# State-space and dilated block on one Trainium2 core: six projections as plain float32 products, by halves of the heads

## The chip, the cores and the metric

The program runs on one core of one Trainium2 chip. The metric is the device time of one execution in microseconds. TensorE (PE) multiplies matrices and loads its weights beside that (PEld); VectorE (DVE), ScalarE (ACT) and GpSimd (POOL) work on elements; SyncE (SP) issues the loads of the weights.

## What is computed

A first block (gated recurrence, attention, routed experts) is followed by a second block of two layers. The change lies in the first layer of the second block. For 256 tokens `x` of 1024 features that layer computes:

```python
h = rmsnorm(x, pre_norm[layer])
proj = h @ w_in                      # 1024 x 5120
q, k, v, g_att, u_ssm, g_ssm = jnp.split(proj, cuts, axis=-1)   # 4 x 1024, 2 x 512
q = apply_partial_rope(q, pos) * HEAD_DIM ** -0.5    # 16 heads of 64
k = apply_partial_rope(k, pos)
att = dilated_attention(q, k, v)     # causal; keys at offsets of three dilations; one softmax
ssm = s5_ssm(u_ssm, ...)             # 32 groups of 16 channels, 64 complex states each, then a GLU
merged = jnp.concatenate([att * silu(g_att), ssm * silu(g_ssm)], axis=-1)
x = x + rmsnorm(merged @ w_out, post_norm[layer])
```

## The kernel before

The layer is written in `even2` (from line 2062). Weights come by `wload` (line 169) as chunks `wch` of 1 MB: four blocks of 128 rows by 512 columns, two chunks for a projection of 512 columns. `rows` takes them to `split` (line 175) by halves of a chunk: ACT casts the half to float32r, the high part `wh` (line 188), and DVE subtracts it from the weight, the low part `wl` (line 189). The input is in two parts as well, `h` high and low, made by `gain_T` (line 456): ACT multiplies the transposed tokens by the gain (line 467), DVE makes the rest. `mm3` (lines 209 to 211) then forms high x high, high x low and low x high. `proj2` (line 2043) gives 512 columns by feature: 96 products of 128 weight columns by 256 tokens, named `pj`. `tokm` (line 221) gives 512 columns by token: 48 products of 512 columns, named `pv`.

The layer begins with `gain_T`, the sums of squares of the norm, and the two projections of the state space (columns 4096 and 4608). Then `ssm` (line 2195) goes through four groups `q` of four steps `j`. In a step PE forms `bu` (line 2213), DVE turns it by the rotation table of the group (lines 2218 to 2221: m1 and m2) and scans it (line 2225: z), and POOL turns it back (lines 2227 and 2228). m1, m2 and z are buffers of one ring, tag t2, of `t2b` = 10. At a group's end PE forms `yps` (line 2234), DVE `sy` (line 2236), ACT the gelu. When all four are done, `gl` (line 2241) is a product with unsplit weights, 16 of 128 x 128 by 256.

The rotation tables lie in four units `Eu[0..3]` of 8 KB a partition, one for each group. After the state space the same units hold the queries, keys, gates and values of all 16 heads, one kind in each unit. The attention goes by halves of the heads (`s`): queries and keys (projected, copied by ACT at line 2127, rotated by DVE and POOL in `rope`, line 737), values (ACT, line 2133), gate (DVE line 2108, silu on ACT), then `dil_pair` (line 2145) for four pairs of heads: scores `sd` (line 2154), mask and maximum on DVE, exp on ACT (line 2168), transposes (line 2180), `ob` (lines 2187 and 2191), and the gated result in two parts `ma`. The output product `yo` follows.

The code is written in this order, and a scheduler sets the order of each engine from what depends on what: products of later projections are issued between those of the state space and of the pairs of heads.

Of the kernel before, what the change touches and what calls it, by code (L numbers as in the profile page):

```python
# [20 lines left out]
P = 128  # L21
# [10 lines left out]
def _consts():  # L32
    """Tables that depend on shapes alone."""
# [53 lines left out]
class Kern:  # L87
# [32 lines left out]
    def consts(self):  # L120
        """what is not needed at the start"""
# [12 lines left out]
        # per token and expert: the token's number in two parts, the weight in three  # L134
# [12 lines left out]
    def unit(self, name, dt=F32):  # L147
        """a unit held from here on, in the order of the loads"""
        t = self.W.tile([P, 2048], dt, name=name, tag="w")
        if dt == F32:  # L150
            o = LAY["half"][0]
            with self.nc.allow_non_contiguous_dma("small"):
                self.nc.sync.dma_start(t[:, :1], self.a["const"][:, o:o + 1])
        else:
            self.nc.gpsimd.tensor_copy(t[:, :1], self.ident[:, :1])
        return t
# [18 lines left out]
    def split(self, v, perm=False, to=None):  # L175
        """f32 [P,k,c] -> two float32r parts whose sum is v; perm: columns (g a d) -> (a g d); to: where they go"""
# [15 lines left out]
    def rows(self, W, K, c0, cn=512, perm=False, got=()):  # L192
        """weight columns c0:c0+cn, row chunk by row chunk (k, high, low); got: loads that are under way"""
# [19 lines left out]
    def feat(self, outs, W, K, c0, x, xs, cn=512, perm=False, chk=False, it=None):  # L213
        """outs[i][128 columns, tokens] = W[:, c0 + 128 i ...].T @ x; x(k) -> high, low [P, tokens]"""
# [6 lines left out]
    def tokm(self, outs, W, K, c0, x, ts, cn=512, chk=False):  # L221
        """outs[i][128 tokens, columns]"""
# [7 lines left out]
    def rsqrt(self, v, shape, scale=1.0):  # L230
        """scale * v**-0.5 of a small tile: a guess on the exponent, then steps of the third and the second order"""
# [17 lines left out]
    def rstd_rows(self, tiles, n, junk):  # L249
        """1/sqrt(mean of squares + eps) of the rows of token tiles; junk: places for the squares, by halves of rows"""  # L250
# [12 lines left out]
    def rstd_of(self, ss, m, n=D):  # L263
        """from the sums of squares of the rows' halves [P, m, 2]"""
# [5 lines left out]
    def squares(self, t, c):  # L270
        """sums of squares of a half of the rows of tile t, for the second layer's norm"""
# [3 lines left out]
    def row_squares(self, ss, tiles, after=None):  # L275
        """ss[:, t, c]: the sums of squares of the halves of the tiles' rows"""
# [6 lines left out]
    def transpose_to(self, src, n, evac):  # L283
        """src(c) [P,128] for c<n, four a bank; evac(q, bank)"""
# [7 lines left out]
    def split_evac(self, hi, lo, src, eng=0):  # L292
        """src (PSUM or SBUF f32) -> hi + lo"""
# [38 lines left out]
    def ada_group(self, layer, i, bank=False):  # L332
        """generator: one weight chunk a step"""
# [43 lines left out]
    def ada_first_setup(self):  # L377
        """gains and shifts of the first norm: their biases, by feature"""
# [10 lines left out]
    def ada_first(self, f):  # L389
        """shift and scale of the features' quarter f for the first norm, both conditions; the row chunks' sums lie in  # L390
        four column groups"""
# [39 lines left out]
    def norm_turn(self, xs, dg, q, tag, bufs):  # L431
        """two row chunks of two token tiles: the transpose, times the row's factor"""
# [16 lines left out]
    def first_rows(self, it, n, pool=True):  # L449
        """the first weights of a phase, split beside the end of the one before"""  # L450
# [5 lines left out]
    def gain_T(self, xs, A, hT, banks, after=None):  # L456
        """x * gain of two token tiles, transposed, in two parts; the rows' factor comes to what the products give"""
        nc = self.nc
        for k in range(8):
# [8 lines left out]
            self.last_lo = nc.vector.scalar_tensor_tensor(lo, src, A[:, k:k + 1], hi.bitcast(F32), op0=OP.mult, op1=OP.subtract).ins  # L468

    def along(self, r, tag, bufs):  # L470
        """the rows' factors r [P, 2] of two token tiles along the free dimension, in every partition"""
# [11 lines left out]
    def router_prep(self, layer, NT):  # L483
        """the router's weights times the gain, what the shift adds, and the rows of shift and gain"""
# [24 lines left out]
    def router_half(self, c, lp, order):  # L509
        """transposes, products and sums of squares of the columns' half c; order: pairs of tiles"""  # L510
# [21 lines left out]
    def x_gain(self):  # L532
        """x * gain"""
# [7 lines left out]
    def router_end(self, lp):  # L541
# [16 lines left out]
        # the experts' affinities  # L558
# [4 lines left out]
    def layer0(self):  # L563
        nc, tc, a = self.nc, self.tc, self.a
        with ExitStack() as st:
# [25 lines left out]
            # by quarters of the features: the first projection's first row chunks wait for the first quarter alone  # L591
# [6 lines left out]
            def quarter(f):  # L598
                """its modulation, and its features of x, transposed"""
# [27 lines left out]
            # the units that the projections fill  # L627
# [66 lines left out]
            # output projection  # L694
# [42 lines left out]
    def rope(self, xv, cos, sin, half=16, eng=None, sin_eng=None):  # L737
        """eng, sin_eng: where the products with the cosines and the sines are done"""
# [22 lines left out]
    def lower_bounds(self):  # L761
        """of layer 0: the first softmax weight of three; and 1 - it, it - 1"""
# [18 lines left out]
    def hgrn(self, HU, v, Y, S2, more):  # L781
# [9 lines left out]
        for h in range(4):  # L791
# [3 lines left out]
            for d in range(2):  # L795
# [31 lines left out]
                # within chunks  # L827
# [5 lines left out]
                # keys by token  # L833
# [5 lines left out]
                # states before each chunk, in the order of the scan  # L839
# [43 lines left out]
    def head_norm(self, y, gain, eng):  # L883
        """rms_norm over each head's 128 columns, in place"""
# [61 lines left out]
    def route(self, NT, CB):  # L946
        """from the logits: each token's two experts, their weights and its rows among them"""
# [3 lines left out]
        # sel: the experts by groups, and the groups' scores behind them  # L951
# [1420 lines left out]
```

## Time and profile before

| | |
|---|---|
| median of 3 runs | 2246.64 us (2244.28 to 2251.62) |
| profiled execution: span (its own time is given by this alone) | 2244.3 us |
| mean granted clock | 0.957 |
| PE busy | 2015.4 us (90%) x11562 |
| PEld busy | 1382.0 us (62%) x11563 |
| DVE busy | 1461.3 us (65%) x2625 |
| ACT busy | 926.2 us (41%) x1377 |
| POOL busy | 340.3 us (15%) x376 |
| `even2` | from 1785 to 2062 us of the span |

The span runs from the first to the last instruction of one profiled execution. Busy time is the time in which an engine has an instruction at work; products overlap in their modelled ends, so the distance between the starts of two tells more than their length. The granted clock is the share of full speed that PE was given. Products of plain float32 leave two records each.

### The profile page before, as it was taken

Reading aid. Unit: us, or ns where it says so; the run is one execution under the profiler, and the core shown is the slowest. Engines: PE = TensorE matmul, PEld = TensorE weight load, DVE = VectorE, ACT = ScalarE, POOL = GpSimd, SP = SyncE. Lnnn points to the kernel's source line nnn. Section 1 sums busy time; section 2 is a strip of 40 time slices with the busy share of each in tenths; the row PEclk is TensorE's granted clock in tenths of the full one; section 3 lists DMA queues with packets and bytes.
Section 4 is the critical chain, followed back from the end, with each engine's and each line's share of the span. In section 5 each row is a group of like instructions: output and inputs, shape, how many; then the busy total and the mean of one; then the engine's idle time right before and its main releaser. Section 6 shows DMA issues by size and latency. Waiting matters only on the chain. (4 is left out here: it accounts for less than half of the span.)

```text
span 2244.3 us, 30379 instructions
## 1 busy us (share of the span) xinstructions
PE 2015.4 (90%) x11562; PEld 1382.0 (62%) x11563; DVE 1461.3 (65%) x2625; ACT 926.2 (41%) x1377; POOL 340.3 (15%) x376
## 2 busy tenths in 40 slices
PE   6997899969999999996989979999888788998998
PEld 2675675647778888774785533333333256786997
DVE  3336778668999999898857545232321288776767
ACT  2222324327778887774645610000000131555443
POOL 1210003040000000016020020011100035221111
PEclk9998999979999999999998989999999978999999
DMA  8854245649999999996532589999999922544560
GB/s 269 276 189 160 70 146 197 241 147 343 367 363 391 382 387 386 381 348 231 188 114 57 208 316 355 395 409 409 409 409 408 366 69 67 188 151 158 167 210 19
DMA packets 187068, 580.53 MB, mean 259 GB/s; under 512 B 18592, under 2 KB 41568, under 8 KB 181792
## 3 DMA queue, kind: packets, MB, share of 16 engines
q1 hardware_dynamic: 172416, 550.02, 66.2%
q0 software_dynamic: 7760, 23.26, 3.3%
q10 hardware_dynamic: 6736, 5.21, 0.8%
q8 instruction: 93, 1.52, 0.3%
q14 instruction: 63, 0.52, 0.1%
HBM read 568.41 MB, written 10.03 MB: 258 GB/s over the span
## 5 line engine op out<-in xcount | busy, mean ns | idle before, releaser
L189 DVE TENSOR_TENSOR wl<-wch,wh 128x1024 fp32r<-128x1024 f32 x534 | 676.3, 1286 | 155.2 <-ACT wh L188 139.4
L188 ACT CAST wh<-wch 128x1024 fp32r<-128x1024 f32 x540 | 562.0, 1052 | 377.8 <-PE pj L210 78.3
L211 PE MATMUL pj<-h,wl 128*128 128x256 f32 x512 | 148.2, 292 | 4.1 <-DVE wl L189 4.1
L209 PE MATMUL pj<-h,wh 128*128 128x256 f32 x512 | 148.7, 292 | 2.5 <-DVE ug L2301 1.2
L210 PE MATMUL pj<-h,wh 128*128 128x256 f32 x512 | 148.7, 291 | 0.0
L1265 PE MATMUL G<-wch,xT 128*64 128x512 f32 x512 | 125.8, 618 | 1.5 <-DMA wch<-in_moe_w_gate_dram 1.2
L1265 PE MATMUL U<-wch,xT 128*64 128x512 f32 x512 | 119.9, 600 | 4.1 <-DMA wch<-in_moe_w_up_dram 3.5
L1279 ACT ACTIVATE s<-G 128x512 f32<-128x512 f32 x16 | 9.6, 597 | 272.7 <-PE G L1265 272.7
L1265 PE MATMUL Y<-wch,hTe 128*64 128x512 f32 x488 | 110.5, 597 | 6.6 <-DMA wch<-in_moe_w_down_dram 5.0
L210 PE MATMUL U<-wl,xu 128*128 128x512 f32 x256 | 103.3, 403 | 9.6 <-DVE wl L189 8.6
L210 PE MATMUL G<-wl,xu 128*128 128x512 f32 x256 | 103.0, 402 | 8.3 <-DVE wl L189 8.0
L210 PE MATMUL Y<-wl,hu 128*128 128x512 f32 x256 | 102.9, 402 | 6.1 <-DVE wl L189 5.8
L211 PEld LDWEIGHTS pj<-h,wl 128*128 128x128 f32 x512 | 99.7, 196 | 9.6 <-DVE wl L189 4.7
L209 PE MATMUL U<-wh,xu 128*128 128x512 f32 x256 | 101.8, 397 | 3.4 <-ACT wh L188 3.4
L209 PEld LDWEIGHTS pj<-h,wh 128*128 128x128 f32 x512 | 100.6, 197 | 6.9 <-issue 3.1
L210 PEld LDWEIGHTS pj<-h,wh 128*128 128x128 f32 x512 | 100.6, 197 | 3.8 <-issue 3.6
L209 PE MATMUL Y<-wh,hu 128*128 128x512 f32 x256 | 100.6, 393 | 2.6 <-ACT wh L188 2.4
L209 PE MATMUL G<-wh,xu 128*128 128x512 f32 x256 | 101.4, 396 | 0.0
L211 PE MATMUL Y<-wh,hu 128*128 128x512 f32 x256 | 100.8, 394 | 0.0
L211 PE MATMUL U<-wh,xu 128*128 128x512 f32 x256 | 100.7, 393 | 0.0
L211 PE MATMUL G<-wh,xu 128*128 128x512 f32 x256 | 100.2, 391 | 0.0
L1232 POOL DMA_INDIRECT xg<-h2d,idx x15 | 18.7, 1244 | 419.3 <-PE tp L1236 403.9
(667 smaller groups left out, 4279.9 us busy)
## 6 DMA issues: line engine op xcount, KB each, us to landing
wch<-in_moe_w_gate_dram SPq DMA_DIRECT2D x128, 1024.0 KB, 7.7
wch<-in_moe_w_up_dram SPq DMA_DIRECT2D x128, 1024.0 KB, 9.0
wch<-in_moe_w_down_dram SPq DMA_DIRECT2D x125, 1024.0 KB, 7.7
wch<-in_ada_w_dram SPq DMA_DIRECT2D x40, 1024.0 KB, 6.0
wch<-in_even_w_in_dram SPq DMA_DIRECT2D x34, 1024.0 KB, 5.6
wch<-in_odd_w_in_dram SPq DMA_DIRECT2D x16, 1024.0 KB, 5.5
wch<-in_even_w_out_dram SPq DMA_DIRECT2D x10, 1024.0 KB, 6.3
wch<-in_ada_w_dram SPq DMA_DIRECT2D x32, 256.0 KB, 6.6
```

Of the source, the lines that this page charges most:

```text
L188: self.last_h = nc.scalar.copy(h, v).ins
L189: self.last_l = e.tensor_tensor(l, v, h.bitcast(F32), op=OP.subtract).ins
L209: m(out, lh, rh, start=first, stop=False, skip_group_check=chk)
L210: m(out, lh, rl, start=False, stop=False, skip_group_check=chk)
L211: self.last_m = m(out, ll, rh, start=False, stop=last, skip_group_check=chk).ins
L1232: nc.gpsimd.indirect_dma_start(out=xg[:], out_offset=None, in_=h2d[:, :], in_offset=bass.IndirectOffsetOnAxis(ap=idx[:, e:e + 1], axis=0))
L1265: self.last_m = nc.tensor.matmul(out[f * 64:f * 64 + 64, :], x[:, k, :], v[k - k0][:, f * 512:(f + 1) * 512], start=(k == 0), stop=(k == 7 ...
L1279: self.last_s = nc.scalar.activation(s, G, AF.Silu).ins
```

## The change

A method `plain` forms the projection by feature from unsplit chunks, a method `plain_tok` the one by token. Their input is `xw`, the transposed tokens times the gain in one float32 part, which `gain_T` makes with one more ACT instruction for each of eight blocks. `xw` takes 8 KB a partition, and the ring t2 has 9 buffers instead of 10. The two projections of the state space and the output product stay split. Each half of the heads now has two units of its own: queries and keys in `Eu[2s]`, values and gate in `Eu[2s + 1]`. The code's order is: queries of half 0, values and gate of half 0, queries of half 1, pairs 0 to 3, values and gate of half 1, pairs 4 to 7. (The two units `ma` are taken after the queries of half 1.) `dil_pair` indexes its unit by `jl = j % 4`.

```diff
+    def plain(self, outs, W, K, c0, x):
+        for k0 in range(0, K, 4):
+            v = self.wload(W, k0, 4, c0, 512)
+            for k in range(4):
+                for i, o in enumerate(outs):
+                    self.nc.tensor.matmul(o, v[:, k, i * P:(i + 1) * P], x[:, k0 + k], start=k0 + k == 0 and not i % 2, stop=k0 + k == K - 1,
+                                          skip_group_check=True)
+    def plain_tok(self, outs, W, K, c0, x):
+        for k0 in range(0, K, 4):
+            v = self.wload(W, k0, 4, c0, 512)
+            for k in range(4):
+                for t, o in enumerate(outs):
+                    self.nc.tensor.matmul(o, x[:, k0 + k, t * P:(t + 1) * P], v[:, k], start=k0 + k == 0, stop=k0 + k == K - 1)
...
-    def gain_T(self, xs, A, hT, banks, after=None):
+    def gain_T(self, xs, A, hT, banks, after=None, whole=None):
...
             self.last_lo = nc.vector.scalar_tensor_tensor(lo, src, A[:, k:k + 1], hi.bitcast(F32), op0=OP.mult, op1=OP.subtract).ins
+            if whole is not None:
+                nc.scalar.mul(whole[:, k], src, A[:, k:k + 1])
...
-            self.t2b = 10
+            self.t2b = 9
...
-            self.gain_T(xs, self.fpg, hT, (("tp", 1), ("bu", 2), ("bu", 2), ("pj", 4), ("pj", 4)), self.last_h)
+            xw = wk.tile([P, 8, 256], F32, name="xw", bufs=1)
+            self.gain_T(xs, self.fpg, hT, (("tp", 1), ("bu", 2), ("bu", 2), ("pj", 4), ("pj", 4)), self.last_h, xw)
...
             self.ssm(uT, gs, ms)
-            qT, kT, ga = (v8(self.Eu[i]) for i in range(3))
-            v = self.Eu[3].rearrange("p (t c) -> p t c", t=2)
+            def plain2(c0):
+                b = [ps.tile([P, 2, 256], F32, name="pj", tag="pj", bufs=4) for _ in range(2)]
+                self.plain([b[i // 2][:, i % 2] for i in range(4)], W, 8, c0, xw)
+                return b
+            def queries(s):
+                u = v8(self.Eu[2 * s])
+                for c0, dst in ((0, u[:, :4]), (1024, u[:, 4:])):
+                    for i, b in enumerate(plain2(c0 + s * 512)):
+                        nc.scalar.copy(dst[:, 2 * i:2 * i + 2], b)
+                        for m in range(2):
+                            self.rope(dst[:, 2 * i + m], cosb, sinb, half=8, eng=nc.gpsimd, sin_eng=nc.gpsimd)
+                return u[:, :4], u[:, 4:]
+            def values(s):
+                u = self.Eu[2 * s + 1]
+                v, ga = u[:, :1024].rearrange("p (t c) -> p t c", t=2), v8(u)[:, 4:]
+                o = [ps.tile([P, 512], F32, name="pv", tag="pj", bufs=4) for _ in range(2)]
+                self.plain_tok(o, W, 8, 2048 + s * 512, xw)
+                for t in range(2):
+                    nc.scalar.mul(v[:, t], o[t], rf[:, 2 + t:3 + t])
+                for i, b in enumerate(plain2(3072 + s * 512)):
+                    g = scaled(ga[:, 2 * i:2 * i + 2], b)
+                    nc.scalar.activation(g, g, AF.Silu)
+                return v, ga
+            h0 = queries(0) + values(0)
+            qk = queries(1)
             ma = [v8(self.unit("ma%d" % i, F32R)) for i in range(2)]
-            for s in range(2):
-                for c0, dst in ((0, qT), (1024, kT)):
-                    for i, b in enumerate(self.proj2(x, W, 8, c0 + s * 512, "pj", 4)):
...
-                for j in range(s * 4, s * 4 + 4):
-                    self.dil_pair(j, qT, kT, v, ga, dil, ma)
+            for j in range(4):
+                self.dil_pair(j, *h0, dil, ma)
+            h1 = qk + values(1)
+            for j in range(4, 8):
+                self.dil_pair(j, *h1, dil, ma)
```

Where the order of the engines moves, three places are shown. The first is ACT at the gain stage, before (`wh` is a cast of weights, `h_14963` the high part of the input, `sq` and `sqg` the squares of the norms):

```order
L188 CAST wh<-wch 128x1024 x2
L467 ACTIVATE h_14963<-tp,fpg 128x256 x7
L188 CAST wh<-wch 128x1024
L467 ACTIVATE h_14963<-tp,fpg 128x256
L281 ACTIVATE sq,nss<-xin 128x512 x4
L188 CAST wh<-wch 128x1024
L2089 ACTIVATE sqg,nss<-sqg 128x512 x4
L188 CAST wh<-wch 128x1024 x3
```

The same place now:

```order
L188 CAST wh<-wch 128x1024 x2
L485 ACTIVATE h_14963<-tp,fpg 128x256 x3
L488 ACTIVATE xw<-tp,fpg 128x256
L485 ACTIVATE h_14963<-tp,fpg 128x256
L488 ACTIVATE xw<-tp,fpg 128x256 x3
L485 ACTIVATE h_14963<-tp,fpg 128x256 x3
L488 ACTIVATE xw<-tp,fpg 128x256
L485 ACTIVATE h_14963<-tp,fpg 128x256
L488 ACTIVATE xw<-tp,fpg 128x256 x3
L298 ACTIVATE sq,nss<-xin 128x512 x4
L188 CAST wh<-wch 128x1024
L2110 ACTIVATE sqg,nss<-sqg 128x512 x4
```

Eight instructions for `xw` have come in, and the third cast, which stood before the last part of the input, stands behind the first squares.

The second place is DVE in the state space, at a border between two groups (m, z and sy as above), before:

```order
L2218 TENSOR_TENSOR m_15447<-bu,rotE_12498 128x512
L2219 TENSOR_TENSOR m_15448<-bu,rotE_12498 128x512
L189 TENSOR_TENSOR wl<-wch,wh 128x1024
L2220 TENSOR_TENSOR m_15447<-m_15447,m_15448 128x256
L2221 TENSOR_TENSOR m_15447<-m_15447,m_15448 128x256
L2225 SCALAR_TENSOR_TENSOR z<-rho,m_15447 128x256 x2
L2218 TENSOR_TENSOR m_15481<-bu,rotE_12500 128x512
L189 TENSOR_TENSOR wl<-wch,wh 128x1024
L2219 TENSOR_TENSOR m_15482<-bu,rotE_12500 128x512
L2236 SCALAR_TENSOR_TENSOR sy<-ug,dsk,yps 128x256
```

And now:

```order
L2257 TENSOR_TENSOR m_15456<-bu,rotE_12498 128x512
L2258 TENSOR_TENSOR m_15457<-bu,rotE_12498 128x512
L2259 TENSOR_TENSOR m_15456<-m_15456,m_15457 128x256
L2260 TENSOR_TENSOR m_15456<-m_15456,m_15457 128x256
L2264 SCALAR_TENSOR_TENSOR z<-rho,m_15456 128x256 x2
L2257 TENSOR_TENSOR m_15490<-bu,rotE_12500 128x512
L2258 TENSOR_TENSOR m_15491<-bu,rotE_12500 128x512
L2275 SCALAR_TENSOR_TENSOR sy<-ug,dsk,yps 128x256
```

The subtractions `wl` have gone from between the steps; the rest keeps its order.

The third place is PE from the end of the state space to the scores of the first pair of heads, now (`yps` is the state space's last product, `sd` the first scores, which used to follow 144 pj, 48 pv and 10 gl):

```order
L2273 MATMUL yps<-m_15608,LCb 32x256
L235 MATMUL pj<-xw,wch 128x256 x3
L2280 MATMUL gl<-yT,wch 128x256 x2
L235 MATMUL pj<-xw,wch 128x256 x4
L2280 MATMUL gl<-yT,wch 128x256 x8
L235 MATMUL pj<-xw,wch 128x256 x19
L244 MATMUL pv<-wch,xw 128x512 x16
L235 MATMUL pj<-xw,wch 128x256 x96
L2193 MATMUL sd<-rotE_12496 128x128 x2
L2193 MATMUL sd<-rotE_12496 128x256 x2
L244 MATMUL pv<-wch,xw 128x512 x2
```

The gate of half 0 and the queries and keys of half 1 (96 pj) all stand ahead of the first scores; between the pairs of half 0 only the values of half 1 and five pj are left to fill in.

## Rows read from the trace of the kernel before

**Rows 1.** Stretches: start:end length, busy us (count) by engine, clock, DMA share, GB/s

```profile
1785.00:1821.00 36.00, 30.80 (x226) 28.62 (x226) 25.61 (x48) 17.59 (x35) 6.88 (x9) 0.91 0.57 191
1821.00:1909.10 88.10, 71.17 (x345) 43.29 (x341) 75.75 (x106) 11.99 (x15) 48.00 (x35) 0.73 0.13 42
1909.10:1947.40 38.30, 33.67 (x213) 30.39 (x212) 28.33 (x49) 17.55 (x24) 15.65 (x16) 0.99 0.64 220
1947.40:1980.70 33.30, 32.56 (x219) 25.02 (x218) 27.67 (x83) 21.25 (x51) 4.86 (x6) 1.00 0.29 96
1980.70:2012.30 31.60, 30.40 (x208) 28.05 (x207) 20.76 (x28) 13.22 (x15) 8.12 (x11) 1.00 0.49 167
2012.30:2062.00 49.70, 49.65 (x234) 35.15 (x233) 34.98 (x94) 27.16 (x60) 3.09 (x4) 1.00 0.38 127
```

**Rows 2.** Timeline, PE, 1913 to 1917 us: start, us, engine, line, op, out<-in, count

```profile
1913.06 0.28 PE L211 MATMUL pj<-h,wl 128*128 128x256 f32 x1
1913.18 0.28 PE L209 MATMUL pj<-h,wh 128*128 128x256 f32 x1
1913.30 3.62 PE L2241 MATMUL gl<-yT,wch 128*128 128x256 f32 x16
1916.57 0.47 PE L210 MATMUL pj<-h,wh 128*128 128x256 f32 x1
```

**Rows 3.** Timeline, PE, products of 512 columns of the values

```profile
1919.74 0.40 PE L210 MATMUL pv<-wl,h 128*128 128x512 f32 x1
1919.97 0.39 PE L211 MATMUL pv<-wh,h 128*128 128x512 f32 x1
```

**Rows 4.** Waits, PE, 1909 to 2012.3 us: us in total, times, longest us

```profile
PE pv L210 <- DVE wl L189: 3.0, 2, 1.8
PE pj L211 <- DVE wl L189: 2.8, 2, 1.9
```

**Rows 5.** Line 2241's instructions, whole span: ns min/median/max, first and last start

```profile
L2241 PE MATMUL gl<-yT,wch x32: 377/379/381, 1897.4 to 1916.5; 128*128 128x256 f32 x32
```

**Rows 6.** Timeline, PE, plain products of an expert

```profile
1338.87 1.89 PE L1265 MATMUL Y<-wch,hTe 128*64 128x512 f32 x8
1340.59 1.89 PE L1265 MATMUL Y<-wa,hTe 128*64 128x512 f32 x8
```

**Rows 7.** DMA issues, 1785 to 2062 us: count, KB each, median us to landing

```profile
wch<-in_even_w_in_dram SPq DMA_DIRECT2D x20, 1024.0 KB, 5.4
```

**Rows 8.** Groups, ACT, 1785 to 1821 us: busy us, mean ns | idle before, releaser

```profile
L467 ACT ACTIVATE h<-tp,fpg 128x256 fp32r<-128x256 f32 x8 | 3.3, 474 | 0.2 <-PE tp L463 0.2
```

**Rows 9.** Groups, DVE, state space, 1821 to 1909.1 us

```profile
L189 DVE TENSOR_TENSOR wl<-wch,wh 128x1024 fp32r<-128x1024 f32 x7 | 12.9, 1841 | 0.1
```

**Rows 10.** Timeline, DVE, first group of the state space and what follows

```profile
1821.36 0.69 DVE L2218 TENSOR_TENSOR m<-bu,rotE 128x512 f32<-128x512 f32 x1 [0.36 <-PE bu L2213]
1823.36 1.26 DVE L2225 TENSOR_TENSOR_SCAN z<-rho,m 128x256 f32<-128x256 f32 x2
1836.13 1.26 DVE L2225 TENSOR_TENSOR_SCAN z<-rho,m 128x256 f32<-128x256 f32 x2
1842.88 0.48 DVE L2236 SCALAR_TENSOR_TENSOR sy<-ug,dsk,yps 128x256 f32<-128x256 f32 x1 [1.34 <-PE yps L2234]
1843.28 1.27 DVE L2225 TENSOR_TENSOR_SCAN z<-rho,m 128x256 f32<-128x256 f32 x2
```

**Rows 11.** Groups, DVE and ACT, 1909.1 to 2012.3 us

```profile
L189 DVE TENSOR_TENSOR wl<-wch,wh 128x1024 fp32r<-128x1024 f32 x27 | 36.8, 1373 | 10.5 <-ACT wh L188 10.5
L188 ACT CAST wh<-wch 128x1024 fp32r<-128x1024 f32 x26 | 27.2, 1048 | 31.6 <-PE pj L210 20.3 <-PE pv L211 9.6 <-DMA wch<-in_even_w_in_dram 1.6
```

**Rows 12.** Stretches of 10 us inside the state space, columns as in rows 1

```profile
1820.00:1830.00 10.00, 5.50 (x21) 2.78 (x19) 9.54 (x16) 2.54 (x3) 3.68 (x3) 0.72 0.01 3
1840.00:1850.00 10.00, 7.83 (x28) 3.45 (x28) 8.53 (x14) 2.30 (x3) 3.97 (x6) 0.50 0.00 0
```

More of the change, by code (lines that the diff above doesn't have):

```diff
@@ L2119, in even2 @@
             self.ssm(uT, gs, ms)
-            qT, kT, ga = (v8(self.Eu[i]) for i in range(3))
-            v = self.Eu[3].rearrange("p (t c) -> p t c", t=2)
-            ma = [v8(self.unit("ma%d" % i, F32R)) for i in range(2)]
-            for s in range(2):
-                for c0, dst in ((0, qT), (1024, kT)):
-                    for i, b in enumerate(self.proj2(x, W, 8, c0 + s * 512, "pj", 4)):
-                        j = s * 4 + 2 * i
-                        nc.scalar.copy(dst[:, j:j + 2], b)
-                        for m in range(2):
-                            self.rope(dst[:, j + m], cosb, sinb, half=8, eng=nc.gpsimd, sin_eng=nc.gpsimd)
-                o = [ps.tile([P, 512], F32, name="pv", tag="pj", bufs=4) for _ in range(2)]
-                self.tokm(o, W, 8, 2048 + s * 512, x, range(2))
-                for t in range(2):
-                    nc.scalar.mul(v[:, t, s * 512:(s + 1) * 512], o[t], rf[:, 2 + t:3 + t])
-                for i, b in enumerate(self.proj2(x, W, 8, 3072 + s * 512, "pj", 4)):
-                    g = scaled(ga[:, s * 4 + 2 * i:s * 4 + 2 * i + 2], b)
-                    nc.scalar.activation(g, g, AF.Silu)
-                for j in range(s * 4, s * 4 + 4):
-                    self.dil_pair(j, qT, kT, v, ga, dil, ma)
@@ L2146, in dil_pair @@
         nc, wk, ps = self.nc, self.wk, self.ps
+        jl = j % 4
         cols = ((0, 128), (128, 256))
@@ L2153, in dil_pair @@
                 r = slice(64 * m, 64 * m + 64)
-                nc.tensor.matmul(sp[m][:, o:o + n], qT[r, j, t * P:(t + 1) * P], kT[r, j, :n], start=True, stop=True)
+                nc.tensor.matmul(sp[m][:, o:o + n], qT[r, jl, t * P:(t + 1) * P], kT[r, jl, :n], start=True, stop=True)
         nm = wk.tile([P, 4], F32, name="nm", tag="nm", bufs=3)
@@ L2184, in dil_pair @@
         for m in range(2):
-            h = 2 * j + m
+            h = 2 * jl + m
             o = ob[64 * m:64 * m + 64]
@@ L2188, in dil_pair @@
         for m in range(2):
[L2189 removed]
+            h = 2 * jl + m
             o = ob[64 * m:64 * m + 64]
             nc.tensor.matmul(o[:, P:], v[:, 1, h * 64:h * 64 + 64], pT[m][:, 2], start=False, stop=True, skip_group_check=True)
[L2192 to L2193 removed]
+        nc.vector.tensor_tensor(ga[:, jl], ga[:, jl], ob, op=OP.mult)
+        self.split_evac(ma[0][:, j], ma[1][:, j], ga[:, jl])
     def ssm(self, uT, gs, mh):
```

3 lines of the change are left out of this document (removed).

## The prediction

> **What bounds the kernel now.** I read the page first: the span is 2244.3 us, and the change touches only `even2`, which I found in the timeline between 1785 and 2062 us. Then I cut that stretch at the landmarks of the program and took the busy time of each engine by stage [rows 1]: the gain stage and the projections of the state space (1785 to 1821), the state space (to 1909.1), the projections of the first half of the heads (to 1947.4), its attention (to 1980.7), the projections of the second half (to 2012.3), and its attention with the output product (to 2062). The reader is to see that two engines set the pace in turn. In the state space DVE is busy 75.75 of 88.1 us; behind it PE is busy 33.67 of 38.3, 32.56 of 33.3, 30.40 of 31.6 and 49.65 of 49.7 us, at a granted clock of 0.99 to 1.00. A busy PE is not yet a full one, so I read the distance between its instructions: the split products (pj) start 0.12 us apart [rows 2], the 512-column ones (pv) 0.23 us [rows 3], without gaps that the timeline shows. Its waits there are few: 3.0 + 2.8 us for low parts `wl` that DVE had not yet made [rows 4].
>
> So the question is whether plain products, which spare ACT and DVE work but take PE longer, are paid where PE is the bound.
>
> **The price of a plain product.** The kernel has one already, of the same shape: `gl`, unsplit weights of 128 columns by 256 columns. The code issues 16, the trace has 32 records [rows 5], so a product leaves two. A batch of 16 records starts at 1913.30, and the next pj stands at 1916.57 [rows 2]: 3.27 us for 8 products and about 0.1 us of start, so **0.42 us** each at full clock, against 3 x 0.12 = 0.36 for the three that it replaces. For 512 columns (plain_tok) no row fits wholly. From below: the experts' products of 64 by 512 columns have 8 records from 1338.87 to 1340.59 [rows 6], 0.215 each and, with the same two records a product, 0.43 us; but their weights are 64 columns wide. From above, and taken: twice `gl`, **0.84 us**, since a row of 128 weights is nearest to it. Three split ones take 3 x 0.23 = 0.69.
>
> The Trainium skill, FP8 and Floating Point Precision, section TensorE Precision Notes, says that a true FP32 product takes four passes through the array. By four passes against the three single ones of the split, a product would cost 0.48 instead of the 0.42 that the row shows; the sum would be some 12 us higher, which is the last of the rivals below.
>
> **Part by part.** Six projections by feature (q, k, gate of two halves) and two by token (v) change: 6 x 96 = 576 pj and 2 x 48 = 96 pv go, 6 x 32 = 192 plain products of 256 and 2 x 16 = 32 of 512 columns come. With them go 32 casts on ACT and 32 subtractions on DVE. The loads stay 16 of 1024 KB; one takes 5.4 us to land [rows 7] and feeds 16 plain products, 6.7 us of PE. So I cost them at nothing: the cover is the load before, at work meanwhile; without it each could show up to 5.4 us. That a weight slot is now freed by PE's last product rather than by DVE's subtraction is hidden by the same cover.
>
> *Gain stage.* Eight more multiplications on ACT make `xw`, of 0.474 us each at most [rows 8], 3.8 us together; in the new order of ACT the third cast stands behind them and the squares. At 1785 to 1821 PE is fed by these casts. Bounds 0 (all hidden in ACT's idle time, 17.59 busy of 36 [rows 1]) and +3.8. I take **+2.0**.
>
> *State space.* DVE sets it, and seven subtractions of 12.9 us lie in it [rows 9]. They do not all count: before group borders DVE waits for POOL and PE anyway. Group 0 has no subtraction, so it gives the price: from the start at 1821.36 to the first scan at 1823.36 2.0 us; three steps to 1836.13, 4.26 each; 6.75 us from there to `sy` at 1842.88; from scan to scan over the border, 1836.13 to 1843.28, 7.15 us [rows 10]. Four groups of this kind: 0.36 + 2.0 + 12 x 4.26 + 3 x 7.15 + 6.75 = 81.7 us against 88.1: **-6.4**. The ring of tag t2 shrinks from 10 buffers to 9, so in the new order m2 of the next group waits for the products `yps` instead of POOL. `sy`, in front of the next sums, waits for the same products already, so I cost it at nothing; at most 0.8 us (`sy` and its issue, my estimate from 1842.88 to 1843.28 doubled) at three borders, +2.4. Bounds of the stage: -12.9, if every subtraction was on DVE's path, and 0, if PE paces it instead.
>
> PE's own work here hardly changes: by the order 144 pj of 0.12 (17.3 us) were in it, and now 38 plain ones (16.0).
>
> *Projections and attention, 1909.1 to 2012.3.* By the order of instructions the three stages had 144 + 129 + 159 = 432 pj and 96 pv: 51.8 + 22.1 (0.23 each) = 73.9 us. Now they have 122 + 5 + 27 = 154 plain products of 256 and 32 of 512 columns: 64.7 + 26.9 = 91.6 us. That is +17.7 on PE, and the waits for `wl`, 5.8 us, go: **+11.9**. The 27 subtractions (36.8 us) and 26 casts (27.2 us) that the trace has there [rows 11] are costed at nothing, since PE ends last here: their cover is PE's own row of products. In the attention of the first half PE has as much to fill in as before (129 x 0.12 = 15.5 us; now 16 x 0.84 + 5 x 0.42 = 15.5, counted in the order), so the softmax chain stays hidden as it was. With 512-column products of 0.43 the part would be -1.2; with everything as costed but the waits kept, +17.7. The ends are -1.2 and +17.7.
>
> *Output product.* 144 products of the form of pv, 0.23 us each [rows 3], on a PE busy 49.65 of 49.7 us: unchanged, 0. What follows is shifted as a whole.
>
> Sum: 2.0 - 6.4 + 11.9 = **+7.5**. The profiled execution takes 2244.3 us and becomes 2251.8. It lies 2.3 us below the median of the runs, 2246.64, which becomes **2254**. About 0.3%, 6.7 us, is what a measurement of this kernel can tell from no change; the forecast lies just past it.
>
> **The rivals.**
>
> *The relief is worth more than the waits that show.* PE's rows overlap in their modelled ends, so short waits for DVE and ACT can hide inside them. For it: 10.5 us of DVE's idle time in front of the subtractions end with a cast, and the two engines pass chunks to each other [rows 11]. Against it: pj stand 0.12 us apart wherever I looked. If another 6 us of such waits go, the time is 2248. The Trainium skill, Perfetto Trace Analysis, section Identifying the Most-Contended Engine, holds matmul busy time a poor measure of how near PE is to its limit, and the busy time of the weight loads a good one. By that this rival gains: PEld is busy 25.02 of 33.3 us in the attention's stage [rows 1], which leaves more room than PE's row.
>
> *Faster: DVE paces the attention too.* From 1909.1 to 2012.3 DVE is busy 28.33 + 27.67 + 20.76 = 76.8 us, and 36.8 of these are subtractions [rows 1, 11]; rotation, softmax and gates wait behind them, and with DVE half empty each pair of heads could end sooner. It decides if over 14 us of PE's time there are hidden waits; with 18 the time is 2236. Against it: PE then had 18 us less of own work than its rows show.
>
> *Slower: the clock in the state space.* Over that stage the granted clock has a mean of 0.73 [rows 1], and from 1840 to 1850 it is 0.50 (the lower level, 1.2 of 2.4 GHz), after ten microseconds in which PE was busy for 5.50; PE is busy 7.83 of those 10 us [rows 12]. No pj runs there, so `bu` and `yps` alone take 0.783 of the time. If the clock stays low throughout, they need 0.783 x 81.7 = 64 us, and 38 plain products of twice 0.42 another 32: 96 us against the 81.7 of my sum, 14 more, 2268. It decides if PE's row at half clock is longer than DVE's.
>
> *Slower: four passes against three.* By 0.48 and 0.92 us the products after the state space cost 154 x 0.06 + 32 x 0.08 = 11.8 us more: 2266. The batch of `gl` [rows 2] speaks against it.
>
> That the change does not do what it says would be a loss of the re-laid order; the order shows the plain products and no subtractions beside them, so it gets no share.
>
> **How the numbers follow.** Forecast 0.55 (its own range 2247 to 2262: the 512-column price, the gain stage's 0 to 3.8 and the state space's border), of which 0.33 slower by over 0.3% (above 2253.4) and 0.22 within. Relief 0.18: 0.16 within, 0.02 faster. DVE pace 0.10, faster (below 2239.9). Clock 0.12 and four passes 0.05, slower. Together faster 0.12, within 0.38, slower 0.50. The range reaches from 2242, which leaves out the DVE case, to 2268, which leaves out the longer half of the clock case: about 0.17 outside.
>
> **What would show it.** In the changed profile: first `bu` at about 1822 to 1823; last `yps` near 1904 to 1905, with scans 4.3 us apart in all groups; plain products 0.42 apart (records 0.21) and those of 512 columns 0.84; first `sd` of the first half near 1974, of the second near 2020; the output's end near 2069. Wrong would be: a granted clock at 0.5 through the state space, plain products at another distance, `sd` of the second half before 2008, or PE waiting for loads of `wch`.

## The result, and the profile after

The changed kernel takes 2265.18 us in the median of four runs (2260.76 to 2269.44), the kernel before 2246.11 beside it. The ratio is 1.0077, with an interval of 1.0054 to 1.0099: slower by 12 to 22 us. The time lies within the range of 2242 to 2268, and slower by over 0.3% was the likelier side; but it lies 11 us above the forecast of 2254, so a sum that was to be +7.5 came out more than twice as large. Each trace below is of one execution, which can lie off the median: that of the changed kernel took 2261.71 us, that of e6 2256.68 (median 2248.86), of e10 2239.95 (2234.37) and of e11 2245.87 (2238.22).

The stretches of the changed kernel, with the columns of [rows 1] and cut at the same landmarks of the program:

```profile
1782.40:1819.40 37.00, 31.62 (x220) 29.34 (x220) 24.57 (x46) 19.67 (x42) 6.97 (x9) 0.86 0.71 243
1819.40:1907.00 87.60, 70.69 (x281) 36.67 (x280) 66.48 (x101) 4.96 (x8) 42.40 (x33) 0.75 0.16 54
1907.00:1977.90 70.90, 70.90 (x297) 56.27 (x296) 20.01 (x52) 13.22 (x22) 18.43 (x26) 1.00 0.44 148
1977.90:2015.90 38.00, 34.58 (x132) 16.86 (x131) 24.63 (x81) 14.87 (x46) 5.91 (x8) 0.91 0.41 139
2015.90:2027.70 11.80, 11.80 (x55) 10.14 (x54) 3.90 (x5) 3.71 (x5) 0.18 (x1) 1.00 0.00 1
2027.70:2077.70 50.00, 49.95 (x234) 35.21 (x234) 31.61 (x90) 23.65 (x57) 2.77 (x4) 1.00 0.26 85
```

The reader is to see three things. DVE is 9 us lighter in the state space (66.48 against 75.75), yet the stage is only about 1 us shorter, at a mean clock of 0.75. PE fills the 70.90 us of projections without a gap. And in the attention of half 0 PE is busy for 34.58 of 38.00 us at a clock of 0.91, where before it was 32.56 of 33.30 at 1.00.

The experiments below are read by the same landmarks, from the timelines of PE and ACT: the cast of the last expert's result (`yh`), the first `bu`, PE's first instruction behind the last `yps`, the first `sd` of half 0, PE's first instruction behind half 0's last `ob`, the first `sd` of half 1, and the first transpose of the next layer. What comes before and after is not the change's: the layer starts 3.2 us earlier in the trace of the changed kernel, and what follows takes 182.5 us instead of 182.1.

| us from landmark to landmark | gain stage | state space | to first scores | half 0's attention | to half 1's scores | rest | sum |
|---|---|---|---|---|---|---|---|
| before | 34.65 | 88.87 | 38.39 | 33.24 | 31.65 | 49.87 | 276.67 |
| the change | 36.97 | 87.65 | 70.91 | 37.93 | 11.85 | 49.99 | 295.30 |
| e1, split weights | 35.72 | 90.95 | 60.88 | 43.87 | 6.07 | 49.50 | 286.99 |
| e2, queries of half 1 later | 36.72 | 81.30 | 43.28 | 28.35 | 43.72 | 49.97 | 283.34 |
| e3, ring of 9 | 35.72 | 90.85 | 38.22 | 33.23 | 31.66 | 49.86 | 279.54 |
| e4, xw by POOL | 37.29 | 83.62 | 70.91 | 37.28 | 11.85 | 49.96 | 290.91 |
| e5, rotation later | 36.71 | 83.57 | 70.91 | 32.56 | 12.72 | 49.98 | 286.45 |
| e6, e1 with e2's order | 35.33 | 93.85 | 36.81 | 33.25 | 31.66 | 49.94 | 280.84 |
| e7, plain q and k of half 0 | 36.70 | 88.62 | 43.75 | 33.23 | 31.66 | 49.93 | 283.89 |
| e8, e7 with products between steps | 36.79 | 85.63 | 36.52 | 33.22 | 31.66 | 49.93 | 273.75 |
| e10, e8 with the gate plain | 36.86 | 84.86 | 30.23 | 31.14 | 33.04 | 49.94 | 266.07 |
| e11, e10 with the values plain | 36.72 | 84.65 | 34.65 | 31.13 | 33.04 | 49.95 | 270.14 |

Between the state space and half 1's scores the kernel before takes 38.39 + 33.24 + 31.65 = 103.28 us and the changed one 120.69: +17.4, where the prediction had +11.9.

### The profile page after: what moved, and what is told of

The parts are those of the page before. It is cut to its first block, busy times and chain, and to the rows that moved or that the text cites. A ratio compares the mean times of both kernels' runs of the same rounds, so it can differ in the third digit from the quotient of the medians.

```text
span 2260.2 us, 29856 instructions
## 1 busy us (share of the span) xinstructions
PE 2032.7 (90%) x11338; PEld 1375.0 (61%) x11339; DVE 1419.8 (63%) x2593; ACT 896.6 (40%) x1353; POOL 332.6 (15%) x376
## 5 line engine op out<-in xcount | busy, mean ns | idle before, releaser
L189 DVE TENSOR_TENSOR wl<-wch,wh 128x1024 fp32r<-128x1024 f32 x502 | 627.2, 1271 | 151.1 <-ACT wh L188 135.5
L188 ACT CAST wh<-wch 128x1024 fp32r<-128x1024 f32 x508 | 528.6, 1053 | 342.7 <-PE mm L211 62.9
L209 PE MATMUL pj<-h,wh 128*128 128x256 f32 x320 | 91.9, 290 | 2.5 <-DVE ug L2340 1.2
L211 PE MATMUL pj<-h,wl 128*128 128x256 f32 x320 | 92.1, 289 | 2.2 <-DVE wl L189 2.2
L235 PE MATMUL pj<-xw,wch 128*128 128x256 f32 x384 | 93.3, 397 | 0.0
L210 PE MATMUL pj<-h,wh 128*128 128x256 f32 x320 | 91.9, 288 | 0.1
L235 PEld LDWEIGHTS pj<-xw,wch 128*128 128x128 f32 x384 | 73.4, 196 | 19.1 <-issue 10.0
L209 PE MATMUL mm<-wh,hTh 128*128 128x256 f32 (+1 forms) x256 | 80.8, 316 | 0.0
```

Of the source, the lines that this page charges most:

```text
L188: self.last_h = nc.scalar.copy(h, v).ins
L189: self.last_l = e.tensor_tensor(l, v, h.bitcast(F32), op=OP.subtract).ins
L209: m(out, lh, rh, start=first, stop=False, skip_group_check=chk)
L210: m(out, lh, rl, start=False, stop=False, skip_group_check=chk)
L211: self.last_m = m(out, ll, rh, start=False, stop=last, skip_group_check=chk).ins
L235: self.nc.tensor.matmul(o, v[:, k, i * P:(i + 1) * P], x[:, k0 + k], start=k0 + k == 0 and not i % 2, stop=k0 + k == K - 1, skip_group_che ...
```

## The experiments

The theory that the prediction left was a **price theory**: plain products cost what they cost and PE sets the pace. Its rivals, drawn from the trace of the changed kernel, were an **order theory** (the queries of half 1, called ahead of the pairs of half 0, bring their rotation ahead of the softmax), a **ring theory** (9 buffers) and a **clock theory** (PE's half clock in the state space).

**e1: the re-laid halves and their order, with split weights.**

```diff
-            self.t2b = 9
+            self.t2b = 10
...
-            xw = wk.tile([P, 8, 256], F32, name="xw", bufs=1)
-            self.gain_T(xs, self.fpg, hT, (("tp", 1), ("bu", 2), ("bu", 2), ("pj", 4), ("pj", 4)), self.last_h, xw)
+            self.gain_T(xs, self.fpg, hT, (("tp", 1), ("bu", 2), ("bu", 2), ("pj", 4), ("pj", 4)), self.last_h)
...
-                b = [ps.tile([P, 2, 256], F32, name="pj", tag="pj", bufs=4) for _ in range(2)]
-                self.plain([b[i // 2][:, i % 2] for i in range(4)], W, 8, c0, xw)
-                return b
+                return self.proj2(x, W, 8, c0, "pj", 4)
...
-                self.plain_tok(o, W, 8, 2048 + s * 512, xw)
+                self.tokm(o, W, 8, 2048 + s * 512, x, range(2))
```

> The re-laid halves and the new order of the code, but with split weights everywhere, no xw and 10 buffers in the ring. Price theory (the plain products are what costs): the projections behind the state space return to about 38 + 32 us, the state space to about 89 us, the kernel to 2246 plus what the order costs. Order theory (the queries of half 1 ahead of the pairs of half 0 put their rotation ahead of the softmax on DVE): the attention of half 0 still takes some 38 us instead of 33.2, with PE idle for about 3 us at its start, total about 2251. If the re-laying itself were the loss, 2260 or more.

Measured: 2256.67 us, ratio 1.0057 (1.0037 to 1.0077), so without a single plain product over half of the loss is there (10.6 us of 19.1). Half 0's attention takes 43.87 us, not 33.2; it holds other products of half 1 than before (the values and half of the gate instead of queries and keys), so the three stretches from the state space to half 1's scores are to be compared together: 110.82 us against 103.28. PE waits there for the masks of the scores (3.6 us, two waits) and for subtractions (6.0 us), and the granted clock is 0.50 for ten microseconds. The price theory alone falls; the order theory had 2251, which is too little.

**e2: the changed kernel, with the queries of half 1 behind the pairs of half 0.**

```diff
             h0 = queries(0) + values(0)
-            qk = queries(1)
...
-            h1 = qk + values(1)
+            h1 = queries(1) + values(1)
```

> The changed kernel with one move: the queries of half 1 are called behind the pairs of half 0. Order theory: the idle 3.4 us of PE at the start of half 0's attention and the fall of the clock behind it go, the way from the first scores of half 0 to those of half 1 gets 4 to 5 us shorter for the same products, total about 2260. Price theory: PE has the same products, so the same time within 1 us, 2265.

Measured: 2253.49 us, ratio 1.0030 (1.0006 to 1.0054), less than either theory had. Its stretches:

```profile
1782.00:1818.70 36.70, 31.48 (x218) 29.02 (x218) 24.52 (x46) 19.68 (x42) 6.71 (x9) 0.86 0.71 245
1818.70:1900.00 81.30, 64.23 (x281) 33.70 (x280) 66.55 (x101) 4.96 (x8) 42.42 (x33) 0.81 0.17 59
1900.00:1943.30 43.30, 43.30 (x169) 31.84 (x169) 14.21 (x38) 8.85 (x16) 12.71 (x18) 1.00 0.44 146
1943.30:1971.70 28.40, 28.32 (x144) 18.03 (x143) 18.59 (x67) 13.00 (x42) 0.00 (x0) 1.00 0.33 113
1971.70:2015.40 43.70, 43.70 (x173) 32.20 (x172) 15.75 (x32) 10.39 (x14) 12.02 (x17) 1.00 0.42 144
```

PE has no gap left behind the state space and stays at full clock: 115.35 us instead of 120.69 from there to half 1's scores. The same run's state space, whose order on PE and DVE is that of the changed kernel, is 6.3 us shorter; the order theory doesn't explain that part, and more on it is said at e3.

**e5: only the rotation of half 1 called later.** PE keeps the projections of half 1's queries ahead of the pairs; `turn` calls the eight rotations of half 1 behind pairs 0 to 3.

```diff
...
                         for m in range(2):
-                            self.rope(dst[:, 2 * i + m], cosb, sinb, half=8, eng=nc.gpsimd, sin_eng=nc.gpsimd)
+                            if s == 0:
+                                self.rope(dst[:, 2 * i + m], cosb, sinb, half=8, eng=nc.gpsimd, sin_eng=nc.gpsimd)
...
+            turn(v8(self.Eu[2]))
             h1 = qk + values(1)
```

> The changed kernel with only the rotation of half 1's queries and keys called behind the pairs of half 0; its projections stay ahead of them, so PE has the same products in nearly the same order. If the rotation in DVE's queue ahead of the softmax is what the order costs: PE's idle 3.4 us and the fall of the clock at the start of half 0's attention go, and from the first scores of half 0 to those of half 1 it takes 44 to 45 us (16 x 0.86 + 32 x 0.43 of products and 16.7 us of the attention's own, from the run with the moved queries) instead of 49.8. If PE lacks products to fill in: 49 to 50 as in the changed kernel.

Measured: 32.56 + 12.72 = 45.28 us instead of 37.93 + 11.85 = 49.78; 2256.03 us, ratio 1.0034 (1.0016 to 1.0051). The timeline of DVE in the changed kernel shows what was in the way (L2199 masks the scores, L2200 takes their maximum; L765 and L768 are the rotation):

```profile
1979.97 0.61 DVE L2199 TENSOR_TENSOR pd<-sd,c_dil 128x128 f32<-128x128 f32 x2
1981.32 0.93 DVE L768 TENSOR_TENSOR rotE<-rotE,rot 128x256 f32<-128x256 f32 x1 [0.74 <-POOL rotE L767]
1982.86 0.43 DVE L768 TENSOR_TENSOR rotE<-rotE,rot 128x256 f32<-128x256 f32 x1 [0.62 <-POOL rotE L767]
...
1985.24 0.93 DVE L768 TENSOR_TENSOR rotE<-rotE,rot 128x256 f32<-128x256 f32 x1 [0.76 <-POOL rotE L767]
1986.79 0.42 DVE L768 TENSOR_TENSOR rotE<-rotE,rot 128x256 f32<-128x256 f32 x1 [0.62 <-POOL rotE L767]
1987.13 0.61 DVE L2199 TENSOR_TENSOR pd<-sd,c_dil 128x128 f32<-128x128 f32 x2
```

And PE at the same place:

```profile
1981.54 2.84 PE L244 MATMUL pv<-wch,xw 128*128 128x512 f32 x6
1987.80 1.64 PE L2193 MATMUL sd<-rotE 64*128 64x128 f32 x4 [3.42 <-DVE pd L2199]
1989.37 2.08 PE L244 MATMUL pv<-wch,xw 128*128 128x512 f32 x2
```

Between the first and the second mask DVE turns four tiles and waits for POOL four times. The buffers of `sd` are two, so PE stands still for 3.42 us; behind that the granted clock is 0.50 (the lower level), and four records of `sd` take 1.64 us where they take 0.92 at full clock. In e5's DVE row the masks of two pairs (L2205 there) stand ahead of the first rotation:

```profile
1979.52 0.62 DVE L2205 TENSOR_TENSOR pd<-sd,c_dil 128x128 f32<-128x128 f32 x2
...
1983.05 0.62 DVE L2205 TENSOR_TENSOR pd<-sd,c_dil 128x128 f32<-128x128 f32 x2 [0.23 <-PE sd L2199]
...
1984.12 0.44 DVE L765 STREAM_SHUFFLE rot<-rotE 128x256 f32<-128x256 f32 x1
```

That the rotation was the hold-up, and not a lack of products, is shown: PE's order is nearly the same in both. By the medians e5 and e2 are 9.2 and 11.7 us faster than the change, and this stretch gives 4.5 and 5.3 of it. In the traces the state space gives 4.1 and 6.3 more, by its clock (see e3), which the edits do not touch.

**e6: split weights, re-laid halves, e2's order.** The edits of e1 and e2 together.

> Split weights everywhere, the re-laid halves, and the queries of half 1 behind the pairs of half 0: what is left of the change is the layout of the units. Order theory: as the kernel before, projections and attention 103 us behind the state space, total 2244 to 2249. Layout theory (other times at which units come free delay loads or rotation): as the run with split weights and the change's order, 2254 or more.

Measured: 2248.86 us, ratio 1.0003 (0.9986 to 1.0020); half 0's attention and the way to half 1's scores are 33.25 and 31.66 us, as before, and the three stretches take 101.72 us against the 110.82 of e1, so with split weights the order costs 9.1 us there. The layout of the units costs nothing that can be told. The order of the code does.

**e3: the kernel before with 9 buffers.**

```diff
-            self.t2b = 10
+            self.t2b = 9
```

> The kernel before with one number changed: 9 buffers in the ring t2 instead of 10. Ring theory: at each of the three group borders of the state space the first product m1 of the next group waits for POOL as in the changed kernel; border 1 gets 0.7 us longer, and if the ring is also behind the long second border of the changed kernel (12.9 us from scan to scan), that border grows by several us here too: total +2 to +7, 2248 to 2253. Clock theory (the second border is long because the plain products run at half clock ahead of yps): each border at most 1 us longer, total 2246 to 2249.

Measured: 2246.28 us, ratio 1.0004 (0.9982 to 1.0027). In the traces the three borders take 7.81, 7.86 and 6.66 us from scan to scan instead of 7.15, 7.54 and 5.88, so the ring costs 0.3 to 0.8 us at each, 1.8 in all, which the times can't tell from nothing. The second border in e3:

```profile
1866.84 0.69 DVE L2218 TENSOR_TENSOR m<-bu,rotE 128x512 f32<-128x512 f32 x1 [2.39 <-POOL m L2228]
1868.02 0.69 DVE L2219 TENSOR_TENSOR m<-bu,rotE 128x512 f32<-128x512 f32 x1 [0.49 <-PE yps L2234]
```

The several microseconds at the second border, the larger part of the ring theory, fall. What is behind the long second border in the changed kernel is seen by laying its DVE row and that of e2 side by side. The changed kernel:

```profile
1856.02 1.26 DVE L2264 TENSOR_TENSOR_SCAN z<-rho,m 128x256 f32<-128x256 f32 x2
1859.94 0.69 DVE L2257 TENSOR_TENSOR m<-bu,rotE 128x512 f32<-128x512 f32 x1 [2.66 <-POOL m L2267]
1866.17 0.69 DVE L2258 TENSOR_TENSOR m<-bu,rotE 128x512 f32<-128x512 f32 x1 [5.53 <-PE yps L2273]
1867.86 0.48 DVE L2275 SCALAR_TENSOR_TENSOR sy<-ug,dsk,yps 128x256 f32<-128x256 f32 x1 [1.00 <-PE yps L2273]
```

e2, where the same instructions have other line numbers:

```profile
1855.40 1.26 DVE L2263 TENSOR_TENSOR_SCAN z<-rho,m 128x256 f32<-128x256 f32 x2
1859.33 0.69 DVE L2256 TENSOR_TENSOR m<-bu,rotE 128x512 f32<-128x512 f32 x1 [2.67 <-POOL m L2266]
1860.02 0.69 DVE L2257 TENSOR_TENSOR m<-bu,rotE 128x512 f32<-128x512 f32 x1
1860.87 0.48 DVE L2274 SCALAR_TENSOR_TENSOR sy<-ug,dsk,yps 128x256 f32<-128x256 f32 x1 [0.16 <-PE yps L2272]
```

PE up to that border's `yps` (the row of nine records), first in the changed kernel and then in e2:

```profile
1853.19 2.07 PE L2252 MATMUL bu<-ug,LB 32*128 32x256 f32 x4
1855.19 2.08 PE L235 MATMUL pj<-xw,wch 128*128 128x256 f32 x4
1857.20 1.06 PE L2273 MATMUL yps<-m,LCa 128*32 128x256 f32 x2
1858.19 2.07 PE L235 MATMUL pj<-xw,wch 128*128 128x256 f32 x4
...
1864.20 1.49 PE L2273 MATMUL yps<-m,LCa 128*32 128x256 f32 x9
```

```profile
1855.40 1.13 PE L235 MATMUL pj<-xw,wch 128*128 128x256 f32 x4
...
1858.57 1.18 PE L2272 MATMUL yps<-m,LCa 128*32 128x256 f32 x9
```

In the changed kernel's trace PE is at half clock here and two plain products take twice as long. `bu`, two plain products and the `yps` of a step take PE 5.00 us (1853.19 to 1858.19), more than the 4.28 us in which DVE does a step, so PE falls behind and, counted from the start of the stage, reaches the border's `yps` 5.0 us later than in e2. The clock rose some 49 us into the stage, in e2's some 34 us into it. As m2 of the next group now waits for `yps` (the ring), the delay reaches DVE: 5.53 us. Four kernels whose order on PE, DVE and POOL in the state space is the same (the change, e2, e4, e5) took 87.65, 81.30, 83.62 and 83.57 us for it, at mean clocks of 0.75, 0.81, 0.82 and 0.82. Why the clock rises earlier in one execution than in another no row here shows.

**e4: xw made by POOL.**

```diff
-                nc.scalar.mul(whole[:, k], src, A[:, k:k + 1])
+                nc.gpsimd.tensor_tensor(whole[:, k], hi.bitcast(F32), lo.bitcast(F32), op=OP.add)
```

> The changed kernel, with xw made by POOL as the sum of the two parts that are there already, instead of by eight more ACT instructions. If ACT's extra instructions are what delays the first projections: the first bu comes 34.7 us after the cast yh as before the change, not 37.0, total 2.3 less, about 2263. If the order of the casts or DVE is what delays them: no change of that distance.

Measured: 2261.92 us, ratio 1.0079 (1.0062 to 1.0096); the distance is 37.29 us. It doesn't tell the two apart, since the move brought a cost of its own (last section). Kernels with `xw` have 36.7 to 37.3 us here and those without 34.65 to 35.72. Part of the spread is the clock: without `xw` it is 34.65 us at a mean clock of 0.90 (before) and 35.33 to 35.72 at 0.86 (e1, e3, e6), with `xw` mostly 36.7 to 37.0 at 0.86. At the same clock `xw` so costs some 1 to 1.6 us. PE's waits in the changed kernel have two for `wl` there, 0.9 us together, that the kernel before has not; what makes those late stays open.

**e7: plain products only for the queries and keys of half 0**, with e2's order.

```diff
             def plain2(c0):
+                if c0 not in (0, 1024):
+                    return self.proj2(x, W, 8, c0, "pj", 4)
...
-                self.plain_tok(o, W, 8, 2048 + s * 512, xw)
+                self.tokm(o, W, 8, 2048 + s * 512, x, range(2))
```

> The run with the moved queries, with plain products only for the queries and keys of half 0, the ones that PE forms beside the state space; all else split. Price theory: the state space keeps its gain (81 to 84 us by the clock, instead of 88.9), the gain stage its loss of 1 to 2, and behind the state space 26 plain products and 32 + 16 x 3 split ones are left to the first scores, some 41 to 44 us instead of 38.4, then as before the change: total 2241 to 2247. If the subtractions for values and gate, which now come late, hold PE up: 2250.

Measured: 2251.57 us, ratio 1.0020 (1.0005 to 1.0036). The way to the first scores is 43.75 us, with a wait of 3.7 us for a subtraction of the values; behind that all is as before the change. The total is that of the expectation's second case, the way to the first scores lies within the first case's 41 to 44. In the profiled execution the clock came up late in the state space too (0.75, 88.62 us), so its gain isn't in this trace, and the run doesn't tell how much of the miss is that and how much the wait.

**e8: e7, with the plain products issued between the steps.** A generator issues four of them behind each step from the second on.

```diff
...
+            it = ahead()
-            self.ssm(uT, gs, ms)
+            self.ssm(uT, gs, ms, lambda n: [next(it, None) for _ in range(4)] if n >= 1 else None)
...
                 zs.append((zc, zn))
+                if fill:
+                    fill(i)
```

> As the run with plain products only for queries and keys of half 0, but with four of them issued behind every step of the state space from the second one on, so that all 64 lie beside it. Clock theory (the state space is longer or shorter by when the granted clock rises, and PE at work brings it up earlier): clock 1.00 from about 25 us into the stage on, stage 80 to 85 us, and the first scores 27 to 30 us behind it instead of 38.4: total 2230 to 2238. If the clock stays at 0.5: a step takes 4 x 0.86 + 3.1 = 6.5 us instead of 4.3, the stage 95 us or more, total 2245 or more.

Measured: 2245.74 us, ratio 0.9989 (0.9970 to 1.0009), a miss on both sides: the total is that of the second case, the stage is not. The clock is 1.00 in the stage's first 10 us and lies between 0.66 and 0.81 in the next three tens, the mean 0.86; the stage takes 85.63 us. But to the first scores it takes 36.52 us, not 27 to 30: PE waits 4.9 us for two subtractions of the gate, and the mean clock there is 0.91.

**e10 and e11: the gate of half 0 plain too, then its values as well.** Half 1 stays split.

```diff
-                if c0 not in (0, 1024):
+                if c0 not in (0, 1024, 3072):
```

> As the run with four products issued behind each step of the state space, with the gate of half 0 plain as well, so that no subtraction of the gate is waited for ahead of the first scores. If those waits (4.9 us) and the lower clock behind them were what kept that way at 36.5 us: 4.3 + 11.2 + 32 x 0.43 = 29 to 31 us, half 0's attention and the projections of half 1 as before, total 2236 to 2241, below both kernels. If the splits of half 1 take their place as what PE waits for: 2245.

```diff
-                self.tokm(o, W, 8, 2048 + s * 512, x, range(2))
+                if s == 0:
+                    self.plain_tok(o, W, 8, 2048, xw)
+                else:
+                    self.tokm(o, W, 8, 2048 + s * 512, x, range(2))
```

> As the run before this one, with the values of half 0 plain too: half 0 wholly plain, half 1 split. DVE has no subtraction left in the state space (three, 4 us, lay in it), PE pays 16 x 0.86 - 48 x 0.23 = 2.7 us more behind it. If DVE paces the state space: stage 80 to 83 us at a clock that rises early, way to the first scores 32 to 33 us, total 2235 to 2241, equal to the run before within 2 us. If PE paces it: 2 to 3 us more than that run.

Measured: e10 2234.37 us, ratio 0.9944 (0.9924 to 0.9965); e11 2238.22 us, ratio 0.9964 (0.9949 to 0.9979); the kernel before took 2244.20 beside them. **e10 beats both kernels**, the one before by 10 us in the medians (8 to 17 by the interval), the changed one by about 30 by the two ratios. It is the first case of the expectation, with a total 1.6 us below its range. Two stretches of e10, the state space and the way to the first scores:

```profile
1827.10:1911.90 84.80, 70.99 (x329) 44.13 (x328) 69.60 (x104) 8.59 (x12) 45.02 (x33) 0.88 0.16 56
1911.90:1942.20 30.30, 30.30 (x139) 25.52 (x138) 19.64 (x42) 12.02 (x19) 14.29 (x18) 1.00 0.34 109
```

The products of half 0's queries and keys lie beside the state space, and 30.30 us of products without a gap are left. The state space of e11 (84.65 us) is no shorter for the three subtractions it spares. Its scans stand 4.3 us apart in all groups, where e10 has two steps of 5.4, but its first border takes 9.51 us instead of 6.66, with a wait of m2 for `yps` of 2.51 us. So DVE alone doesn't pace the stage there, and neither case of the expectation fits. PE pays for the plain values behind it: 34.65 instead of 30.23 us. The intervals of the two ratios overlap, so that e10 is the faster of the two is likely, not shown.

## Why the prediction came out as it did

That the time lies within the range is in part luck: the forecast's own range ended at 2262, and the range reached 2268 for a low clock through the whole state space and for the four passes, not for a softmax chain that holds PE up.

**Gain stage, +2.0: the number right, the reason not shown.** It is +2.3 in the trace of the change, but some 1.1 of that is the clock (0.86 there and 0.90 before; e1 and e3 have it without `xw`), and that ACT is behind the rest isn't shown.

**State space, -6.4: DVE's row right, a wait for PE missed.** It came out at -1.2, and at -7.6 in e2. DVE's own row behaves as worked out: scans 4.2 to 4.3 us apart (one step of 4.7), 81.3 us in all where the clock comes up early. The three borders, for which the sum had 7.15 us each, took 7.82, 12.91 and 6.61 in the changed kernel. The step that failed is "`sy`, in front of the next sums, waits for the same products already, so I cost it at nothing; at most 0.8 us": m2's wait for `yps` cost 5.53 us at the second border, because plain products stand ahead of `yps` and PE's row of a step is longer than DVE's at half clock (5.00 against 4.28 us). That is the condition of the clock rival; it came true for part of the stage, not for the whole.

**Projections and attention, +11.9: +17.4 measured.** The step that failed is "In the attention of the first half PE has as much to fill in as before ..., so the softmax chain stays hidden as it was": the products were counted, but not that the rotation of half 1 stood in DVE's queue ahead of the softmax. That the order moves work on DVE too could be read beforehand; only PE's order was looked at there. It cost 4.5 us by e5 and 5.3 by e2.

The prices are not behind the miss, though they were low. The changed kernel's own rows give that of a plain product:

```profile
1914.45 8.37 PE L235 MATMUL pj<-xw,wch 128*128 128x256 f32 x38
1922.66 13.90 PE L244 MATMUL pv<-wch,xw 128*128 128x512 f32 x32
1936.39 8.80 PE L235 MATMUL pj<-xw,wch 128*128 128x256 f32 x40
```

19 products in 8.21 us are 0.432 each, 16 in 13.73 us are 0.858. The lower bound of 0.43 for 512 columns was far off, the doubling of `gl` was right. The sum was short on the split side as well: next to a product of another kind a `pj` took about 0.1 us longer, split (0.22 from start to start instead of 0.12) or plain (0.32 a record instead of 0.22). PE's busy time with `pj` and with `pv` over the three stretches, in the kernel before and then in e2:

```profile
1909.10:2012.30 103.20, 58.69 (x432) 1.00 0.48 164
1909.10:2012.30 103.20, 22.73 (x96) 1.00 0.48 164
1900.00:2015.40 115.40, 71.18 (x308) 1.00 0.40 137
1900.00:2015.40 115.40, 27.79 (x64) 1.00 0.40 137
```

That is 81.4 and 99.0 us, modelled ends included; from start to start it is 78.7 and 96.3, where the sum had 73.9 and 91.6. Both terms were some 5 us short, which cancels by luck, and the difference of +17.6 is the predicted +17.7. With the order put right, e2's trace gives 115.35 - 103.28 = +12.1, and its whole layer +6.7, close to the predicted +11.9 and +7.5: the arithmetic of PE held where PE really was the bound. The +6.7 leans on a state space that is the shortest of the four with the same order; with the 83.6 us of e4 and e5 it would be +9.

**Output product, 0: right** (49.99 against 49.87). So were the loads: PE never waited for one of `wch` in the changed kernel's projections.

**The rivals.** That the relief is worth more than the waits that show, and that DVE paces the attention, both fall: where PE has no waits left (e2) its products go up by +17.6 us and its idle time goes down by 6.5, from 6.57 us to 0.08, little more than the 5.8 of waits that showed. The Trainium skill, Perfetto Trace Analysis, section Identifying the Most-Contended Engine, trusts the busy time of the weight loads; by it, 25.02 of 33.3 us [rows 1] left room that these runs did not find (in e2 the weight loads are busy for 18.03 of the 28.40 us of that stage, and PE for 28.32), and the distance between products was the better measure. Four passes against three (the Trainium skill, FP8 and Floating Point Precision, section TensorE Precision Notes) gives an estimate of 0.48 at the 0.12 us that a split product takes; measured is 0.432, so the count of passes is no price by itself.

## What to carry to other kernels

Plain float32 products trade DVE and ACT time for PE time, 0.43 us for 0.36 here, so they belong where PE waits (beside the state space) and not where it is the bound. e10 keeps the ones beside the state space, and behind it the gate of half 0, whose split form had PE wait 4.9 us (e8). When calls are moved, read the queue of every engine that takes part, since what moves ahead of a softmax on DVE can stop PE, and a stopped PE can pay again through its clock (0.50 behind the 3.42 us). And a term that rests on a stage at varying clock deserves a range of its own.

## What had not been expected

For the same instructions the clock's rise within the state space came some 15 us later in the changed kernel's trace than in e2's, and the stage took 87.7 and 81.3 us. And DVE is slower beside POOL's adds in e4: the four multiplications of DVE's row take 5.77 us while POOL adds `xw`, against 2.49 in the changed kernel, where POOL has none of it. The rows at e5 show the like in the changed kernel: L768 takes 0.93 us while POOL multiplies and 0.42 to 0.43 while it doesn't. First e4, then the change:

```profile
1801.02 5.77 DVE L2108 TENSOR_TENSOR sqg<-xin,gains 128x512 f32<-128x512 f32 x4
```

```profile
1795.62 2.49 DVE L2108 TENSOR_TENSOR sqg<-xin,gains 128x512 f32<-128x512 f32 x4
```
